# An instruction scheduler's cost table re-measured: lengths taken from spacings in the trace, a port charge and table loads counted in an operation's length

## The chip, the cores and the metric

The kernel runs on one core of a Trainium2 chip. The core has five engines, each with its own queue, worked off strictly in order: TensorE (matrix products), VectorE, ScalarE (activation functions), GpSimd, and SyncE, which here only issues DMA transfers. In profiles they are called PE (and PEld for the loading of stationary operands), DVE, ACT, POOL and SP. The metric is the device time of one execution in microseconds, taken as the median over several runs.

## The reference

A two-layer model on 256 tokens of width 1024, all in fp32. Each layer is: half a gated feed-forward block, a mixer, half a feed-forward block, each with a root-mean-square norm before and after it:

```python
for i in range(DEPTH):
    g = norm_g[i]
    h = h + 0.5 * rms_norm(swiglu(rms_norm(h, g[0]), ffn_w1[i, 0], ffn_w2[i, 0]), g[1])
    u = rms_norm(h, g[2])
    m = conv_ssd_mixer(...) if i % 2 == 0 else dilated_attention_mixer(...)
    h = h + rms_norm(m, g[3])
    h = h + 0.5 * rms_norm(swiglu(rms_norm(h, g[4]), ffn_w1[i, 1], ffn_w2[i, 1]), g[5])
```

The feed-forward width is 2816. Layer 0's mixer is a hybrid. One branch is `silu(layer_norm(conv31(val * sigmoid(gate))))`, with a depthwise convolution over 31 tokens and 1024 channels. The other is a state-space branch with 16 heads of 64 and two chunks of 128 tokens: a convolution over 4 tokens, softplus step sizes, products masked by exponential decays, and a gate `silu(z)`. Both are joined by one output product. Layer 1's mixer is attention with 8 heads in three dilation groups, merged by their softmax sums.

## The kernel before, in words

**Stages.** `run` (L1165) records six stages one after another: feed-forward, hybrid mixer, feed-forward, feed-forward, attention, feed-forward. Activations are kept transposed (`xT`), in two tiles of 128 tokens. Every large product is made of three passes: each operand is split into a high part, rounded to the fp32r format (ScalarE writes it, named `wh` for weights), and a remainder (`wl`, a subtraction on VectorE), and `mm3` and `feat_major` multiply high by high, high by low and low by high.

**Weights.** They stream in units of 128x2048 (1 MB): SyncE loads `raw`, ScalarE copies it to `wh`, VectorE subtracts to `wl`. Units 38 to 60 (`GPSIMD_UNITS`, L44), which belong to the hybrid mixer and the start of the next feed-forward block, have the subtraction on GpSimd in pieces of 512 columns instead (L542). There are 4 buffers each for `raw`, `wh` and `wl`.

**The hybrid mixer** (`hybrid`, L787) has the most kinds of work. The long convolution (`long_conv`, L806) is 240 `scalar_tensor_tensor` operations on VectorE that accumulate into two PSUM banks, `t` and `c`, in two groups; they are the taps. They are recorded 2000 places later than they stand in the program (L821), so VectorE fills with them. Next to them run the step sizes (`step_sizes`, L750: some 16 operations on 32 columns that end in tile `a`, with two Exp activations), the decays (`decays`, L875: a mask product on GpSimd, a matmul, Exp on ScalarE, a product on VectorE; for the first chunk also small copies into `left`), the state-space products, and their normalization (the scaling `v<-v,m,g`). At the end the convolution's result goes through a layer norm over channels, from L988 on: products with a tile `mean`, squares, 32 one-column products, a power on GpSimd, two products that spread the result, Silu, a split, and then the last big products.

**Order of issue.** Nothing is issued as it is written. `Recorder` takes down all operations with their dependences and then makes a list schedule (`schedule`, L317). It keeps, for each engine, the time at which it becomes free, and for each operation the time at which its inputs are ready. For each engine `choose` (L346) looks at all operations that could start: the start `s` is the later of those two times, and later still if a buffer has no place yet. Among the operations that could start within `LOOK` of the earliest one (50 ns on TensorE, 100 on VectorE and ScalarE, 0 on GpSimd and SyncE, L425) it takes the one with the lowest rank, its place in the program. Of all engines' choices the one with the earliest start is issued, and its length, `o.cost`, is added (L390). `cost` (L429) has the lengths, in ns, by engine, operation and size; `latency` (L463) the delay from one operation's end to the start of one that needs it. So a length decides nothing by itself: it moves the times at which others can start, and with them the order in each queue, the GpSimd pieces' places in it, and which buffer each tile is given. All instructions are issued from one line, L418, which is therefore the line of nearly every row of the profile.

Of the kernel before, what the change touches and what calls it, by code (L numbers as in the profile page):

```python
# [17 lines left out]
P = 128  # L18
# [30 lines left out]

# ---------------------------------------------------------------- weight order  # L50
def _unit_a(cols512):
# [113 lines left out]

# ------------------------------------------------------------ order of issue
class View:
    """A region of a buffer that has no place yet: the path of view operations, and the region it names in the first buffer of its kind."""

# [23 lines left out]
    def pieces(self):  # L193
        """The parts of the buffer it touches."""
        dims = self.ap.ap[1:]
        at = np.array([self.ap.offset % self.buf.cols])
        for step, n in dims:
            at = (at[:, None] + step * np.arange(n if step else 1)).ravel()
        return np.unique(at // self.buf.grain).tolist()
# [18 lines left out]
class Kind:  # L218
    """Buffers of one size that take turns in the same places."""

# [24 lines left out]
class Recorder:  # L245
    """Takes the program down, then issues it engine by engine in the order of a list schedule."""

# [61 lines left out]
    @contextmanager  # L309
    def moved(self, ranks):  # L310
        """What is recorded inside counts as so many places later."""
        before = self.offset
        self.offset += ranks
        yield
        self.offset = before

    def schedule(self):  # L317
# [28 lines left out]
        def choose(e):  # L346
            found = []
            low = None
            for o in cands[e]:
                s = max(free[e], ready[o.index])  # L350
                if e == "scalar" and o.table and o.table != table:
                    s += TABLE_LOAD
                for b in o.bufs:
                    if b.slot is None:
                        t = place_time(b)
                        if t is None:
                            break
                        s = max(s, t + GAP)
                else:
                    found.append((o.rank, s, o))  # L360
                    if low is None or s < low:
                        low = s
            if low is None:
                return None
            return min((f for f in found if f[1] <= low + LOOK[e]), key=lambda f: f[:2])

        while len(order) < len(ops):
# [11 lines left out]
            for b in o.bufs:  # L379
                if b.slot is None:  # L380
# [8 lines left out]
                    b.last = 0.0  # L389
            free[e] = s + o.cost  # L390
            if e == "sync":
                bus = max(bus, s + DMA_START) + o.tail
                end[o.index] = bus + DMA_LATENCY
            else:
                end[o.index] = s + o.cost
            o.start, o.end = s, end[o.index]
# [23 lines left out]

TABLE_LOAD = 1300.0
GAP = 100.0
# [6 lines left out]
def cost(op, out):  # L429
    """Time on the engine, in ns, and for a transfer its time on the wires."""  # L430
    kw = op.kw
    op.table = None
    n = out.free_size() if isinstance(out, View) else 0
    if op.engine == "tensor":
# [3 lines left out]
        if stationary.ap.dtype == F32R:  # L438
            return max(n, 256) / 2.4 + 2.5, 0.0
        return max(2 * n, 2 * stationary.free_size()) * 2 / 2.4, 0.0  # L440
    psum = any(isinstance(a, View) and a.buf.kind.psum for a in (*op.args, *kw.values()))
# [4 lines left out]
    if op.engine == "gpsimd":  # L446
        if op.name == "memset":
            return 100.0, 0.0
        return (464.0 if n == 1 else 2.15 * n + 60.0), 0.0
    if op.engine == "vector":  # L450
        if op.name == "tensor_scalar" or op.name == "tensor_copy":
            return (0.52 if not psum else 1.04) * n + (70.0 if n < 64 else 130.0), 0.0
        if op.name == "scalar_tensor_tensor":
            return 1.03 * n + (130.0 if n > 64 else 75.0), 0.0
        if op.name == "tensor_reduce":
            n = op.kw["in_"].free_size()
# [11 lines left out]

# --------------------------------------------------------------------- program
class Kernel:  # L470
# [33 lines left out]

    # ---- storage
    def keep(self, name, shape, dtype=F32):
# [19 lines left out]

    # ---- weights
    def split(self, hi, lo, src, engine=None):
# [28 lines left out]

    # ---- matrix products: a, b are (hi, lo) pairs
    def mm3(self, out, a, b, start, stop):
# [38 lines left out]
    def to_transposed(self, src, hi_of, lo_of, n, banks="tc", gain=None):  # L598
        """src: list of [P, 512] token-major pieces; transposes n blocks into split operands."""
        nc = self.nc  # L600
# [18 lines left out]

    # ---- norms  # L620
    def rstd(self, sums, eps):
# [11 lines left out]
    def post_pre(self, t, y, half, gpost, gpre, xT, last=False):  # L633
        """h += f * rms(y) * gpost, then the transposed split of rms(h) * gpre."""
        with self.nc.moved(-HURRY):
# [31 lines left out]

    # ---- gated pairs: func(first) * second
    def gated_tok(self, xT, func, consume, bank="t", first=False):
# [30 lines left out]
    def gated_feat(self, xT, func):  # L700
        """[feature block, token] products of one pair of units."""
        first, second = self.unit(256), self.unit(256)
# [7 lines left out]

    # ---- ffn
    def ffn(self, xT, done):
# [35 lines left out]

    # ---- hybrid mixer
    def step_sizes(self, xT):  # L750
        """softplus step sizes and their decays, [token, (chunk, head)]."""
        nc = self.nc
# [34 lines left out]
    def hybrid(self, xT, done):  # L787
# [4 lines left out]

        # input of the long depthwise convolution, [channel, token]
        glu = []
# [41 lines left out]

        # short convolutions of the state-space branch, [channel, token]
        def xbc_pair(j):
# [16 lines left out]

        # decays between tokens of a chunk, [source, head, target], and score masks
        after, upto = self.order[:, 0, :], self.order[:, 1, :]
        cb = self.slot([P, NT, 2, P])
        for t in range(NT):
# [3 lines left out]
            V.tensor_tensor(out=cb[:, t], in0=pc, in1=upto.unsqueeze(1).to_broadcast([P, 2, P]), op=ALU.mult)  # L863
        # B of the first chunk, [token, state], and the decay since the start of the second
        pb, pg = self.ps([P, 2, P], "a"), self.ps([P, 16], "a")
# [36 lines left out]

        # inputs of the state-space branch, [token, channel]
        xs = [[None, None] for _ in range(NT)]
# [15 lines left out]

        # gate z, [token, channel]; outputs per chunk and group; the state after the first chunk feeds the second
        zu = [[self.unit(512), self.unit(512)] for _ in range(2)]
# [61 lines left out]

        # layer norm of the long convolution over channels
        pm, pv, pr = (self.ps([P, n], tag) for n, tag in zip((SEQ, NT, SEQ), LN_BANKS))
# [42 lines left out]

    # ---- attention mixer  # L1030
    def attention(self, xT, done):
# [216 lines left out]
```

## Time and profile before

| | |
|---|---|
| median of 3 runs | 1151.29 us (1149.3 to 1154.03) |
| span of the profiled execution | 1150.6 us |
| mean granted TensorE clock | 0.992 |
| instructions | 17628, of them 7192 matmuls |
| table loads on ScalarE | 14 |

The span is from the profiled execution's first to its last instruction; the profile states no other time of that execution. In the rows, an instruction is written as engine, line, operation, output tile, inputs, and shapes; names such as `w`, `a`, `t`, `c` are PSUM tiles, and `cv`, `s`, `pt`, `v`, `m` tiles in SBUF. In a view by stretches each engine's busy microseconds stand in the order of its heading, with the number of instructions behind them. In the timeline a row starts with its start and length in microseconds; what stands in brackets is the engine's idle time before it and what ended it. In a view of waits the numbers are the total, the times and the longest. In groups the numbers behind the bar are the busy time, the mean duration in ns, and idle time before. Durations overlap a little from one instruction to the next, so that the spacing of a series is shorter than the duration of one.

### The profile page before, as it was taken

The page shows a single profiled execution, that of the slowest core. Times are in us where ns is not written, and L with a number is a line of the kernel's source. Part 1 is how long each engine was busy: PE and PEld are TensorE (multiplying, and loading weights), DVE is VectorE, ACT ScalarE, POOL GpSimd, SP SyncE. Part 2 cuts the span into 40 slices and gives each one's busy share as a digit, 9 for nine tenths or more (in the row PEclk, how much of TensorE's full clock was granted, in tenths as well). Part 3 has the DMA queues.
Part 4 walks back from the last instruction along what each step waited for, and adds up shares of the span by engine and source line. Part 5 has one row for each costly group of instructions (what it writes and reads, how often), then busy time and mean ns, then how long its engine had stood idle before and what let it go on. Part 6 is the DMA issues. An engine that isn't in the chain of part 4 may idle for free.

```text
span 1150.6 us, 17628 instructions
## 1 busy us (share of the span) xinstructions
PE 1111.9 (97%) x7192; PEld 997.6 (87%) x7192; DVE 689.4 (60%) x1085; ACT 570.0 (50%) x960; POOL 161.8 (14%) x147
## 2 busy tenths in 40 slices
PE   6999999999999899999999999999999999999997
PEld 5899998798777678999988999998999987999996
DVE  5645446799899376355468455458556457554553
ACT  7634435656754455344455344445565566444442
POOL 0000000378887420000000000001000000000000
PEclk9999999999999799999999999999999999999999
DMA  9755454535324346555546555555634413655521
GB/s 333 267 184 183 163 204 147 196 134 186 108 82 159 112 179 219 183 183 179 189 147 238 202 190 180 187 183 175 235 110 154 147 73 125 224 181 185 189 105 37
DMA packets 29921, 197.21 MB, mean 171 GB/s; under 512 B 3600, under 2 KB 4496, under 8 KB 7312
## 3 DMA queue, kind: packets, MB, share of 16 engines
q1 hardware_dynamic: 29840, 196.09, 48.6%
q8 instruction: 56, 0.92, 0.3%
q14 instruction: 25, 0.20, 0.1%
HBM read 195.03 MB, written 1.05 MB: 170 GB/s over the span
## 4 chain that ended last, share of the span: by engine, by line
PE 61%; DVE 1%; ACT 1%; issue 1%; POOL 0%; DVEq 0%; POOLq 0%; ACTq 0%
PE w L418 40%; PE a L418 19%; PE t L418 1%; PE c L418 1%; ACT s L418 0%; ACT wh L418 0%; DVE wl L418 0%; DVE y L418 0%; ACT junk L418 0%; POOL m L418 0%; DVE h L418 0%; DVE x L418 0%; DVE s L418 0%; ACT x L418 0%; POOL wl L418 0%
## 5 line engine op out<-in xcount | busy, mean ns | idle before, releaser
L418 DVE TENSOR_TENSOR wl<-raw,wh 128x1024 fp32r<-128x1024 f32 x310 | 371.5, 1226 | 268.9 <-ACT wh L418 268.7
L418 PE MATMUL w<-x,wh 128*128 128x256 f32 x2912 | 528.0, 283 | 0.9 <-DVE pt L418 0.6
L418 ACT ACTIVATE wh<-raw 128x1024 fp32r<-128x1024 f32 (+1 forms) x402 | 367.3, 955 | 255.7 <-PE w L418 152.3
L418 PEld LDWEIGHTS w<-x,wh 128*128 128x128 f32 x2912 | 454.6, 191 | 5.2 <-issue 1.0
L418 PE MATMUL w<-x,wl 128*128 128x256 f32 x1456 | 412.1, 283 | 0.0
L418 PEld LDWEIGHTS w<-x,wl 128*128 128x128 f32 x1456 | 278.2, 191 | 0.3 <-issue 0.3
L418 PE MATMUL a<-wh,s 128*128 128x512 f32 x768 | 248.2, 397 | 2.0 <-ACT s L418 2.0
L418 PEld LDWEIGHTS a<-wh,s 128*128 128x128 f32 x768 | 145.1, 189 | 35.5 <-ACT s L418 2.7
L418 PE MATMUL w<-wh,x 128*128 128x512 f32 x480 | 156.1, 400 | 4.8 <-ACT x L418 2.7
L418 PE MATMUL a<-wl,s 128*128 128x512 f32 x384 | 151.9, 395 | 0.0
L418 POOL TENSOR_TENSOR m<-m,mhalf 128x1 f32<-128x1 f32 (+1 forms) x27 | 19.2, 712 | 930.0 <-DVE m L418 930.0
L418 POOL TENSOR_TENSOR wl<-raw,wh 128x512 fp32r<-128x512 f32 x92 | 118.9, 1332 | 39.1 <-ACT wh L418 36.2
L418 PEld LDWEIGHTS w<-wh,x 128*128 128x128 f32 x480 | 90.7, 190 | 27.3 <-ACT x L418 3.6
L418 ACT ACTIVATE sg<-w 128x256 f32<-128x256 f32 x96 | 36.3, 378 | 156.7 <-PE w L418 156.7
L418 PE MATMUL w<-wl,x 128*128 128x512 f32 x240 | 95.0, 397 | 0.9 <-POOL wl L418 0.9
L418 DVE TENSOR_TENSOR cv<-sg,w 128x256 f32<-128x256 f32 x76 | 31.8, 418 | 94.0 <-ACT sg L418 94.0
L418 PEld LDWEIGHTS a<-wl,s 128*128 128x128 f32 x384 | 72.6, 189 | 15.6
L418 DVE SCALAR_TENSOR_TENSOR t<-cv,chan,t 128x255 f32<-128x255 f32 (+29 forms) x120 | 56.0, 466 | 3.5 <-ACT t L418 3.1
L418 DVE SCALAR_TENSOR_TENSOR c<-cv,chan,c 128x255 f32<-128x255 f32 (+29 forms) x120 | 55.9, 466 | 0.3 <-ACT c L418 0.2
L418 PEld LDWEIGHTS w<-wl,x 128*128 128x128 f32 x240 | 45.6, 190 | 11.3 <-POOL wl L418 1.7
L418 DVE TENSOR_TENSOR y<-a,g 128x512 f32<-128x512 f32 x24 | 16.4, 684 | 37.1 <-ACT junk L418 37.1
L418 ACT ACTIVATE s<-cv 128x512 fp32r<-128x512 f32 (+1 forms) x44 | 25.6, 594 | 16.0 <-DVE cv L418 16.0
(132 smaller groups left out, 733.7 us busy)
## 6 DMA issues: line engine op xcount, KB each, us to landing
raw<-in_weights SPq DMA_DIRECT2D x176, 1024.0 KB, 4.9
g<-in_gains SPq DMA_DIRECT2D x12, 512.0 KB, 4.3
raw<-in_weights SPq DMA_DIRECT2D x4, 512.0 KB, 8.6
h<-in_x SPq DMA_DIRECT2D x2, 512.0 KB, 6.2
out<-h SPq DMA_DIRECT2D x4, 256.0 KB, 2.1
s<-in_consts SPq DMA_DIRECT2D x3, 192.0 KB, 2.4
chan<-in_chan SPq DMA_DIRECT2D x1, 166.0 KB, 8.5
order<-in_consts SPq DMA_DIRECT2D x1, 128.0 KB, 9.3
```

Of the source, the lines that this page charges most:

```text
L418: o.ins = f(*[real(a) for a in o.args], **{k: real(a) for k, a in o.kw.items()})
```

## The change

Only `schedule` and `cost` change in effect (the rest of the diff removes comments and docstrings). In `schedule`, the test for a table load no longer delays the start of an operation in `choose`; it stands where the chosen operation's length is worked out. An operation of VectorE that has no PSUM operand (`shares_port`) gets, also after it has been chosen, the rest of the GpSimd operation that the plan has running at its start. In `cost`, the lengths of fp32r and fp32 products, GpSimd operations, and `scalar_tensor_tensor` without a pointer are new; `bn_stats` and `bn_aggr` do not occur in this kernel.

```diff
@@ choose
                 s = max(free[e], ready[o.index])
-                if e == "scalar" and o.table and o.table != table:
-                    s += TABLE_LOAD
@@ schedule
-            free[e] = s + o.cost
+            length = o.cost
+            if e == "scalar" and o.table and o.table != table:
+                length += TABLE_LOAD
+            if o.shares_port:
+                length += max(0.0, free["gpsimd"] - s)
+            free[e] = s + length
             if e == "sync":
                 bus = max(bus, s + DMA_START) + o.tail
                 end[o.index] = bus + DMA_LATENCY
             else:
-                end[o.index] = s + o.cost
+                end[o.index] = s + length
@@
-TABLE_LOAD = 1300.0
+TABLE_LOAD = 1294.0
@@ cost
     op.table = None
+    op.shares_port = False
@@ tensor
         if stationary.ap.dtype == F32R:
-            return max(n, 256) / 2.4 + 2.5, 0.0
-        return max(2 * n, 2 * stationary.free_size()) * 2 / 2.4, 0.0
+            return n / 2.4 + 17.0 if n > 256 else 120.0, 0.0
+        return 2 * max(2 * n / 2.4 + 2.5, 112.0), 0.0
@@ gpsimd
-        return (464.0 if n == 1 else 2.15 * n + 60.0), 0.0
+        if n == 1:
+            return 515.0, 0.0
+        return (2.35 if out.ap.dtype == F32R else 1.9) * n + 40.0, 0.0
     if op.engine == "vector":
+        op.shares_port = not psum
@@ scalar_tensor_tensor
-            return 1.03 * n + (130.0 if n > 64 else 75.0), 0.0
-        if op.name == "tensor_reduce":
+            return 1.03 * n + (130.0 if n > 64 and isinstance(kw.get("scalar"), View) else 75.0), 0.0
+        if op.name == "bn_aggr":
+            return 200.0, 0.0
+        if op.name in ("tensor_reduce", "bn_stats"):
             n = op.kw["in_"].free_size()
```

Between the choice and these lines stands, unchanged, L377 and 378: `if e == "scalar" and o.table: table = o.table`.

## The prediction

> **What bounds the kernel now.** I read the page's head first, then busy time by stretches of the span, then the waits of TensorE and VectorE inside the stretch that stood out, then the timeline there.
>
> ```profile
> span 1150.6 us, 17628 instructions
> PE 1111.9 (97%) x7192; PEld 997.6 (87%) x7192; DVE 689.4 (60%) x1085; ACT 570.0 (50%) x960; POOL 161.8 (14%) x147
> ```
> ```profile
> core 0: us, PE busy (x) PEld busy (x) DVE busy (x) ACT busy (x) POOL busy (x), PEclk, DMA share, GB/s
> 0.00:25.00 25.00, 15.25 (x60) 11.75 (x61) 15.12 (x31) 17.55 (x36) 1.56 (x8) 1.00 0.89 320
> 25.00:205.00 180.00, 180.00 (x1204) 165.38 (x1203) 96.12 (x111) 85.99 (x117) 1.10 (x2) 1.00 0.55 194
> 205.00:225.00 20.00, 19.00 (x89) 15.24 (x88) 13.26 (x23) 11.52 (x22) 4.34 (x4) 1.00 0.62 214
> 225.00:373.20 148.20, 137.95 (x859) 117.71 (x857) 141.40 (x336) 84.54 (x159) 121.18 (x100) 0.99 0.39 136
> 373.20:392.00 18.80, 14.08 (x54) 11.68 (x54) 8.32 (x25) 9.68 (x26) 9.96 (x9) 0.64 0.48 169
> 392.00:425.00 33.00, 30.45 (x138) 24.00 (x137) 19.57 (x31) 16.29 (x39) 13.42 (x12) 1.00 0.32 122
> 425.00:825.00 400.00, 399.93 (x2616) 364.74 (x2615) 221.22 (x266) 186.88 (x263) 6.09 (x8) 1.00 0.55 192
> 825.00:970.00 145.00, 140.91 (x1011) 126.49 (x1010) 85.90 (x166) 83.28 (x209) 3.04 (x4) 1.00 0.36 126
> 970.00:1144.00 174.00, 174.00 (x1176) 160.65 (x1174) 85.55 (x94) 73.19 (x94) 0.55 (x1) 1.00 0.44 155
> ```
>
> TensorE is idle for 1150.6 - 1111.9 = 38.7 us in all. The three feed-forward stretches (25 to 205, 425 to 825, 970 to 1144) have 0.07 us of that between them: there TensorE is the only bound, and an order can lose time but not win any. Of the rest, 9.75 us are the start (0 to 25) and 6.3 the end. What an order can win lies in the hybrid mixer: 1.0 us in 205 to 225, 10.25 in 225 to 373, 4.7 in 373 to 392, 2.55 in 392 to 425; and in the attention mixer, 4.1. In 225 to 373 VectorE is even busier than TensorE, 141.40 of 148.20 us. That stretch ends where the long convolution does:
>
> ```profile
> 369.99 1.89 PE L418 MATMUL w<-cv,mean 128*128 128x256 f32 x8
> 372.74 0.46 DVE L418 SCALAR_TENSOR_TENSOR c<-cv,chan,c 128x226 f32<-128x226 f32 x1
> 373.39 1.99 PE L418 MATMUL w<-cv,mean 128*128 128x256 f32 x8 [1.51 <-ACT cv L418]
> 387.74 0.79 PE L418 MATMUL a<-wh,s 128*128 128x512 f32 x1 [2.01 <-ACT s L418]
> ```
>
> VectorE's last tap runs at 372.74; only then can TensorE take the second half of the channel means (373.39), and a serial layer norm follows until the next big product at 387.74. TensorE's other products had run out at 369.99. So two things set when the layer norm starts: VectorE's total until the last tap, and, 3.4 us earlier, TensorE's supply of other work. The layer norm itself is the same operations in the same chain, and its granted clock was 0.64.
>
> **The change, part by part.** No operation is added, removed or resized: 7192 matmuls, 1085 VectorE, 960 ScalarE and 147 GpSimd instructions stay. The order of each queue and the place of each buffer may move, and all of the cost or gain comes from that.
>
> *Matmul lengths.* From the chain of waits:
>
> ```profile
> 462.61 11.50 PE w L418 x96
> 474.11 5.59 PE a L418 x24
> ```
>
> 11.50/96 = 119.8 ns for a 256-column product and 5.59/24 = 232.9 ns for a 512-column one. The old plan used 256/2.4 + 2.5 = 109.2 and 215.8; the new one 120 and 230.3. So the old plan let TensorE run 8 to 9% too fast against engines whose lengths were about right. In 225 to 373 that is an estimated 137.95 x 0.085 = 11.7 us over the stretch. An engine's queue is strict in order, so an operation planned too early holds up what is ready behind it. On VectorE what is behind it is nearly always a tap of the convolution. What this cost so far is in VectorE's waits of that window:
>
> ```profile
> DVE s L418 <- ACT s L418: 3.1, 4, 1.4
> DVE t L418 <- ACT t L418: 3.1, 2, 2.8
> ```
>
> These two are 6.2 of the 148.20 - 141.40 = 6.8 us that VectorE is idle there. If the plan is right, taps fill such gaps and the last tap comes up to 6.8 us earlier; if it is not, nothing comes. I take 5, since the 3.1 us on t is the start of a group of taps, which partly stays. TensorE must then run out of other work earlier as well; it has 10.25 us of idleness in the window, of which these two are the largest:
>
> ```profile
> PE a L418 <- ACT s L418: 3.8, 3, 2.8
> PE w L418 <- DVE pt L418: 2.3, 3, 0.9
> ```
>
> 5 us more on VectorE asks for 5 - 3.4 = 1.6 of those 10.25: not the limit.
>
> *GpSimd lengths and the port.*
>
> ```profile
> 222.60 15.01 POOL L418 TENSOR_TENSOR wl<-raw,wh 128x512 fp32r<-128x512 f32 x12 [11.72 <-ACT wh L418]
> 234.68 2.98 DVE L418 SCALAR_TENSOR_TENSOR m<-m 128x32 f32<-128x32 f32 x1
> 244.00 4.04 POOL L418 TENSOR_TENSOR s<-m,order 128x512 f32<-128x512 f32 x4 [6.39 <-DVE m L418]
> 275.57 2.51 DVE L418 COPY m<-s 128x4 f32<-128x4 f32 x1
> 278.73 0.16 DVE L418 COPY m<-s 128x4 f32<-128x4 f32 x1
> L418 DVE TENSOR_TENSOR s<-s,s 128x512 f32<-128x512 f32 x8 | 8.3, 1067 | 1.2 <-ACT s L418 0.7
> 278.12 0.69 DVE L418 TENSOR_TENSOR s<-s,s 128x512 f32<-128x512 f32 x1
> L418 DVE SCALAR_TENSOR_TENSOR v<-v,m,g 128x512 f32<-128x512 f32 x4 | 6.9, 1765 | 0.2
> L418 DVE SCALAR_TENSOR_TENSOR h<-y,m,h 128x512 f32<-128x512 f32 x24 | 17.1, 748 | 1.5
> ```
>
> A weight piece takes 15.01/12 = 1.25 us on GpSimd; the old plan had 2.15 x 512 + 60 = 1.16, the new one 2.35 x 512 + 40 = 1.24. A mask product takes 4.04/4 = 1.01; old 1.16, new 1.9 x 512 + 40 = 1.01. The held operations are real: 2.98 us for 32 columns, over as GpSimd's batch ends (222.60 + 15.01 = 237.61); a copy of 2.51 against 0.16; eight decay products at 1.067 against 0.69; four scalings at 1.765 against 0.748. Together (2.98 - 0.2) + (2.51 - 0.16) + 8 x 0.38 + 4 x 1.02 = 12.2 us of VectorE's 141.40. But the change puts this into the length, after the choice: VectorE still takes such an operation when its rank says so, and still stands. I take 0 for these 12.2 us. Bounds: all gone, -12; as much again, +12.
>
> The plan's charge is also not what happens. It runs to the end of the GpSimd operation in progress, at most 1.24 us, while the copy stood 2.35 longer than its twin, through two boundaries of a batch. And it falls on every operation without a PSUM operand, where this one ran freely inside a batch:
>
> ```profile
> 350.22 2.53 POOL L418 TENSOR_TENSOR wl<-raw,wh 128x512 fp32r<-128x512 f32 x2
> 351.12 0.20 DVE L418 TENSOR_SCALAR m<-m 128x1 f32<-128x1 f32 x1
> ```
>
> The Trainium skill (GPSIMD Engine Reference, Key points) limits the contention to VectorE instructions in a 2-port mode or with two SBUF inputs, which speaks against charging the rest. The row of 0.20 us agrees with it, and by it the sum is the same.
>
> *Table loads.* Here the code does not do what the change's name says. The line `table = o.table` (L378) stands between the choice and the new lines and was not moved. When the length is worked out, `o.table != table` is therefore always false, and no load is ever charged. The start no longer holds it either. So in the new plan a load costs nothing, neither in the choice between two operations nor in time.
>
> ```profile
> L418 ACT ACT_TABLE_LOAD x14 | 18.0, 1283 | 8.4 <-DVE s L418 4.2 <-PE a L418 3.3 <-PEq L1238 0.7
> 272.78 0.55 ACT L418 ACTIVATE s<-w,chan 128x256 f32<-128x256 f32 x1
> 273.35 1.28 ACT L418 ACT_TABLE_LOAD   x1
> 274.64 0.18 ACT L418 ACTIVATE m<-a 128x16 f32<-128x16 f32 x1
> 287.10 1.28 ACT L418 ACT_TABLE_LOAD   x1 [3.63 <-DVE s L418]
> 313.93 1.28 ACT L418 ACT_TABLE_LOAD   x1 [3.27 <-PE a L418]
> ```
>
> A switch costs 274.64 - 273.33 = 1.31 us, and what follows one is now planned that much too early. Where ScalarE has work before the load, its slack (148.20 - 84.54 = 64 us in the hybrid's long stretch) takes it up. Where ScalarE had been waiting for the input, as at 287.10 and 313.93, the load lies on a chain, and the engine that comes next stands for it: TensorE waits 3.8 us for s in this window (the row above). I take three such places, 3 x 1.3 = +4. Then the number of loads: the old rule kept a function of another table behind any copy that could start within 1.2 us; now rank alone decides, and Exp and Silu may alternate. Two loads fewer would be -2.6; four more, all on a chain, +5.2; I take 0. The feed-forward stretches use Silu alone, attention Exp alone; one Exp (of `heads`, L773) runs in the first feed-forward block, where TensorE never waits, and may move into the start, where it does: -1.3 to +2.6, taken as 0.
>
> The Trainium skill (ScalarE: Activation LUTs, What ACT_TABLE_LOAD costs) adds a drain of 1.38 us to each switch and comes to about 2.66. The trace disagrees with its 1.31. By the page the three places would be +8 instead of +4.
>
> *The small ones.* fp32 products get 2 x 112 ns where they had 213, scalar_tensor_tensor without a pointer 75 ns where it had 130; power 515 for 464. They shift attention and layer norm by tens of ns each. Attention's stretch is idle for 4.1 us in many short waits; I take 1 of it (bounds 0 to 3 gained, 3 lost). At 392 to 425, where the gated h returns to the feed-forward, I take 1 of 2.55. SyncE's queue holds the same loads; it works on at most 0.62 of the DMA engines' time outside the start (205 to 225), so loads that move by a few us stay covered. The start stays: its waits are on loads and on the first normalization. The feed-forward stretches stay at 0; should a weight piece come late there, nothing covers it, since TensorE has no slack.
>
> Sum against the profiled execution: 1150.6 - 5 + 4 - 1 - 1 = 1147.6. The median of the runs, 1151.29, lies 0.7 above the span, so 1148.3; I say 1148.5. That is less than the 5.75 us (0.5%) that a measurement of this kernel can tell from no change.
>
> **Rivals.** *Faster, by the right pace.* If the free table loads cost nothing because ScalarE's slack takes them all up, the sum is 1144.3. If then TensorE still has products left when the layer norm starts, they cover part of its 4.7 us of idleness in 373 to 392, and some of the time at clock 0.64: another 4, so 1140. For it: 8 to 9% on every product is no rounding, and a TensorE that is planned right moves every queue. Against it: VectorE idles only 4.6% of its stretch, and 12.2 us of its time are port waits that no choice looks at. I put it at 1142.
>
> *Slower, by the port.* Step sizes and decays need some 16 tiny VectorE operations in a row, nearly all without PSUM. So far only the first was held (2.98), since GpSimd then stood idle 6.39 us, waiting for their result. The new plan makes that chain longer, by up to 1.24 us each, and GpSimd takes whatever starts earliest: if it has weight pieces to put into that gap, each tiny operation stands for one. Half a piece for all 16 is 16 x 0.62 = 10 us more on VectorE, which moves the last tap and the layer norm by as much: 1151.3 + 10 = 1161. It decides from about 9 of them held. For it: all of that can be seen in the rows above. Against it: the weight pieces need free buffers, which the old order lacked at 237.61.
>
> *Slower, by free table loads.* If Exp and Silu alternate in the hybrid, eight more loads, half of them on a chain, are 4 x 1.3 = 5.2 beside the 4 above, and the pace gains nothing: 1151.3 + 9 = 1160. It decides from about 18 loads in all. Against it: ranks keep the Exps of one chunk together.
>
> *Nothing done.* The issued orders could come out nearly the same, since ranks make most choices: 1151. With so many ties in time I give that little, inside the forecast's case.
>
> **How the numbers follow.** The forecast, gains and losses that nearly cancel, from 1145.5 to 1157: 0.38. Faster, 1136 to 1145.5: 0.33. Slower, 1157 to 1168: 0.29, of which 0.17 by the port and 0.12 by the loads. The likeliest case's own range is 1145.5 to 1157. The range over all, 1137 to 1164, leaves out about 0.05 below, where the port waits would have to go too, and 0.1 above.
>
> **What would show it.** Right: TensorE still without idleness in the feed-forward stretches; VectorE's idle time before the last tap under 4 us, the last tap at 369 to 373, a layer norm as long as before; longer waits behind two or three table loads. Wrong: the last tap before 366 or after 377; held tiny operations in a row between the step sizes and the decays; more than 16 loads; idleness of TensorE in a feed-forward stretch.

## The result and the profile after

| | before | after |
|---|---|---|
| median | 1151.45 us (4 runs, 1149.3 to 1154.03) | 1162.55 us (4 runs, 1162.23 to 1163.66) |
| span of the profiled execution | 1150.6 us | 1161.9 us |
| mean granted TensorE clock | 0.992 | 0.987 |
| table loads on ScalarE | 14 | 16 |

The ratio is 1.0112, with a 95% interval of 1.0093 to 1.013: 1.1% slower. The head of the page after:

```profile
span 1161.9 us, 17647 instructions
PE 1115.7 (96%) x7192; PEld 997.1 (86%) x7192; DVE 688.5 (59%) x1085; ACT 573.4 (49%) x962; POOL 158.6 (14%) x147
```

The engines do the same work as before, within 4 us each; TensorE's idle time went from 38.7 to 46.2 us. Where it is, the view by stretches of the changed kernel tells, cut at the same events as before:

```profile
core 0: us, PE busy (x) PEld busy (x) DVE busy (x) ACT busy (x) POOL busy (x), PEclk, DMA share, GB/s
25.00:205.00 180.00, 180.00 (x1206) 165.20 (x1205) 97.88 (x112) 86.38 (x116) 1.09 (x2) 1.00 0.55 196
205.00:225.00 20.00, 18.59 (x86) 14.65 (x85) 12.70 (x22) 10.79 (x22) 3.20 (x4) 1.00 0.56 201
225.00:378.83 153.83, 138.82 (x860) 117.63 (x858) 141.58 (x336) 88.49 (x162) 123.81 (x103) 0.99 0.39 138
378.83:400.00 21.17, 16.46 (x53) 13.43 (x54) 8.31 (x25) 9.88 (x27) 6.39 (x6) 0.50 0.30 101
432.00:832.00 400.00, 399.59 (x2612) 363.06 (x2611) 221.91 (x265) 185.60 (x259) 4.93 (x8) 1.00 0.55 194
832.00:981.00 149.00, 140.66 (x1012) 126.41 (x1011) 86.08 (x166) 83.54 (x209) 3.04 (x4) 1.00 0.35 124
981.00:1155.50 174.50, 174.50 (x1179) 160.28 (x1177) 85.52 (x94) 73.25 (x94) 0.55 (x1) 1.00 0.44 154
```

The feed-forward stretches are as full as they were (399.59 of 400, 174.50 of 174.50). Two places are longer. From 225 to the last tap it is 153.83 us where it was 148.20, and VectorE, with the same 336 instructions and nearly the same work (141.58 against 141.40), idles 12.25 us in place of 6.8. In attention TensorE idles 8.3 us in place of 4.1. In the timeline the end of the convolution and the layer norm:

```profile
378.37 0.44 DVE L421 SCALAR_TENSOR_TENSOR c<-cv,chan,c 128x226 f32<-128x226 f32 x1
379.01 3.78 PE L421 MATMUL w<-cv,mean 128*128 128x256 f32 x8 [5.09 <-ACT cv L421]
395.53 0.79 PE L421 MATMUL a<-wh,s 128*128 128x512 f32 x1 [2.01 <-ACT s L421]
```

The last tap comes at 378.37 (372.74 before), TensorE stands 5.09 us for it (1.51 before), and the first big product behind the layer norm is at 395.53 (387.74). From the second means to that product it is now 16.5 us instead of 14.35, at a granted clock of 0.50 in 378.83 to 400. What VectorE waits for ahead of the last tap (total, times, longest):

```profile
DVE t L421 <- ACT t L421: 5.0, 2, 2.8
DVE m L421 <- ACT s L421: 4.0, 3, 1.8
DVE s L421 <- ACT s L421: 2.7, 3, 1.4
```

The second row is new: 4.0 us in which `m` waits for `s` of ScalarE. And in attention, two waits of TensorE for the copy of `cv`, where before had one of 0.33 us at 895.61:

```profile
865.37 0.51 PE L421 MATMUL w<-x,wh 128*128 128x256 f32 x2 [1.48 <-ACT cv L421]
903.27 0.50 PE L421 MATMUL w<-x,wh 128*128 128x256 f32 x2 [1.59 <-ACT cv L421]
```

The new row of VectorE, seen close up. ScalarE, TensorE and VectorE of the changed kernel:

```profile
271.62 1.28 ACT L421 ACT_TABLE_LOAD   x1
273.15 1.12 PE L421 MATMUL a<-s,order 128*128 128x512 f32 x2 [1.39 <-ACT m L421]
274.31 0.60 ACT L421 ACTIVATE s<-a 128x512 f32<-128x512 f32 x1 [0.18 <-PE a L421]
274.93 1.28 ACT L421 ACT_TABLE_LOAD   x1
274.94 1.94 DVE L421 COPY m<-s 128x4 f32<-128x4 f32 x1 [1.81 <-ACT s L421]
276.22 0.63 ACT L421 ACTIVATE s<-s 128x512 f32<-128x512 f32 x1
276.87 1.28 ACT L421 ACT_TABLE_LOAD   x1
276.90 1.16 PE L421 MATMUL a<-s,s 128*128 128x128 f32 x8 [0.93 <-ACT s L421]
278.16 0.60 ACT L421 ACTIVATE s<-a 128x512 f32<-128x512 f32 x1
278.81 3.68 PE L421 MATMUL a<-s,order 128*128 128x512 f32 x4 [0.75 <-ACT s L421]
280.89 0.60 ACT L421 ACTIVATE s<-a 128x512 f32<-128x512 f32 x1 [2.13 <-PE a L421]
281.52 0.17 DVE L421 COPY m<-s 128x4 f32<-128x4 f32 x1 [1.52 <-ACT s L421]
283.16 0.17 DVE L421 COPY m<-s 128x4 f32<-128x4 f32 x1 [0.64 <-ACT s L421]
```

A Silu (`s<-s`) stands between the Exps (`s<-a`) of one chunk, so that three loads fall into 6.5 us. The plan holds them to be free. TensorE stands behind each of them: 1.39 us for the small Exp after the first load (ScalarE's `m`), 0.93 for the Silu after the second, 0.75 for the Exp after the third. The granted clock in 278.8 to 282.5 was then 0.54, and four products with `order` took 3.68 us. The Exps need these products (at 280.89 ScalarE itself has waited 2.13 us for one), and VectorE's copies need the Exps; the plan has set them only 0.1 to 2.5 us behind the ends that it gives the Exps without loads. So VectorE stands at three copies, 1.81 + 1.52 + 0.64 = 3.97 us; the taps behind them could have run. The loads reach it for the greater part by way of TensorE.

### The profile page after: what moved, and what is told of

Same layout as the page of the kernel before. It is cut to its first block, busy times and chain, and to the rows that moved or that the text cites. A ratio compares the mean times of both kernels' runs of the same rounds, so it can differ in the third digit from the quotient of the medians.

```text
span 1161.9 us, 17647 instructions
## 1 busy us (share of the span) xinstructions
PE 1115.7 (96%) x7192; PEld 997.1 (86%) x7192; DVE 688.5 (59%) x1085; ACT 573.4 (49%) x962; POOL 158.6 (14%) x147
## 4 chain that ended last, share of the span: by engine, by line
PE 58%; DVE 3%; ACT 2%; issue 1%; POOL 1%; DVEq 0%; POOLq 0%; ACTq 0%
PE w L421 38%; PE a L421 18%; ACT s L421 1%; PE t L421 1%; DVE y L421 1%; ACT wh L421 1%; DVE h L421 0%; POOL m L421 0%; PE c L421 0%; DVE s L421 0%; DVE x L421 0%; ACT junk L421 0%; DVE wl L421 0%; DVE m L421 0%; POOL wl L421 0%
## 5 line engine op out<-in xcount | busy, mean ns | idle before, releaser
L421 PEld LDWEIGHTS w<-wl,x 128*128 128x128 f32 x240 | 45.7, 191 | 12.2 <-DVE wl L421 1.4
```

Of the source, the lines that this page charges most:

```text
L421: o.ins = f(*[real(a) for a in o.args], **{k: real(a) for k, a in o.kw.items()})
```

## The experiments

Two measures recur. *Lost time* of TensorE is its start-to-start spacings, less what the same shape took in the median of the trace of before; for a single wait that is nearly the bracket in the row. *Planned* times are the starts and ends that the kernel's own list schedule gave its operations; they are no measurements, but they can be laid beside the trace, operation by operation.

The first question was whether the uncounted table loads alone make the loss, or the new product lengths, or the port charge, or whether any new order costs about as much.

**The product lengths alone.** The kernel before, with

```diff
-            return max(n, 256) / 2.4 + 2.5, 0.0
-        return max(2 * n, 2 * stationary.free_size()) * 2 / 2.4, 0.0
+            return n / 2.4 + 17.0 if n > 256 else 120.0, 0.0
+        return 2 * max(2 * n / 2.4 + 2.5, 112.0), 0.0
```

> The kernel before with the new matmul lengths alone (fp32r and fp32). Theory 'free loads': 14 loads; the pace by itself does no harm, 1146 to 1153 (my prediction took -5 to -7 for it). Rival 'lengths': 1157 to 1163, with VectorE's idle time before the last tap over 10 us and attention's 3.8 us with it. Rival 'port charge': 1149 to 1154.

Measured: 1160.66 us, ratio 1.0093 (1.0063 to 1.0123). The last tap came at 365.8, 7 us earlier than before, VectorE waited nowhere for ScalarE's `s` for more than 0.2 us in all, and the kernel was slower nevertheless. TensorE took the means only at 372.71:

```profile
372.71 3.62 PE L418 MATMUL w<-cv,mean 128*128 128x256 f32 x16
```

All 16 in a row and no wait before them: TensorE was the late one. Ahead of them it stood for other things, 10.6 us in 225 to 374.4; in the kernel before these other things were 8.9 us, since 1.51 of its 10.44 us up to 373.4 were the wait for the tap. Between the two profiled executions (before's was a long one in the hybrid, as the last section shows) only 1.0 of the 7.1 us were lost up to the second half of the means. 0.6 followed in the layer norm, 2.9 between it and the first scores of attention, and 1.6 between attention's scores.

**The free table loads alone.** The kernel before without the load in the start:

```diff
-                if e == "scalar" and o.table and o.table != table:
-                    s += TABLE_LOAD
```

> The kernel before, with one edit: choose no longer adds the table load to the start (so loads are free in the plan, as in the changed kernel; all lengths are the old ones). Theory 'free loads' (the Exps of the first chunk are parted by a Silu at 275 us, VectorE's copies stand behind them, the last tap comes 5.6 us later, the layer norm 7.8): 16 loads, waits of VectorE's m on ScalarE's s of about 4 us, last tap 376 to 379, 1157 to 1163. Rival 'lengths' (the new matmul lengths move the queues against each other): 1149 to 1154, last tap within 1.5 us of 372.7. Rival 'port charge': as the rival 'lengths' here.

Measured: 1150.44 us, ratio 1.0001 (0.9985 to 1.0018). 16 loads as in the changed kernel, and VectorE's waits for `s` grew from 3.1 to 5.3 us, but the time did not move. Alone, on the old lengths, free loads cost nothing that can be measured.

**The port charge alone.** The kernel before with `shares_port` and its charge in the length:

```diff
+            if o.shares_port:
+                length += max(0.0, free["gpsimd"] - s)
```

> The kernel before with the port charge alone added to the length of VectorE's operations without PSUM. Theory 'free loads': 1149 to 1154. Rival 'lengths': 1149 to 1154. Rival 'port charge': 1157 to 1163, with more held VectorE operations than before (12.2 us).

Measured: 1152.45 us, ratio 1.0025 (1.0013 to 1.0038).

**The change without free loads.** The changed kernel with the old test back in `choose`, so that a load delays the start again:

```diff
                 s = max(free[e], ready[o.index])
+                if e == "scalar" and o.table and o.table != table:
+                    s += TABLE_LOAD
```

> The changed kernel with the table load back in the start in choose; all the new lengths and the port charge stay. Theory 'free loads': 14 loads, no Silu between the Exps, last tap 369 to 374, 1145 to 1153 (attention's 3.8 us, which have no load in them, may stay: then 1152 to 1155). Rivals 'lengths' and 'port charge': 1159 to 1164.

Measured: 1159.71 us, ratio 1.0088 (1.0053 to 1.0122). The last tap came back to 371.7, and nearly four fifths of the loss stayed. So neither the loads nor any other single part explains the whole, and the parts do not add up: 0.93, 0.01 and 0.25% alone.

The next question was whether the planned pace of TensorE as such does it: a plan that lets TensorE run too fast gives everybody else a lead.

**The change with the old product lengths**, the first diff reversed in the changed kernel.

> The changed kernel with the old matmul lengths (256/2.4 + 2.5 and so on); port charge, free loads and the rest stay. Theory 'matmul lengths' (the right pace itself makes the order worse): 1148 to 1154. Rival 'any new order' (the old order is a lucky one, every change of lengths draws another, usually 0 to 12 us slower): anything from 1149 to 1163.

Measured: 1165.76 us, ratio 1.0138 (1.0113 to 1.0164), above both ranges. TensorE stood 17.5 us for the last tap:

```profile
387.75 3.78 PE L421 MATMUL w<-cv,mean 128*128 128x256 f32 x8 [17.50 <-ACT cv L421]
```

and VectorE had waited ahead of it mostly for ScalarE's `s`:

```profile
DVE s L421 <- ACT s L421: 9.9, 10, 2.8
```

So the new product lengths are no plain harm. Put into the kernel before they lose 0.93%; among the other parts of the change the kernel is no slower with them than without (1.0112 against 1.0138, intervals that overlap).

**The pace alone.** The kernel before with one factor on the length of fp32r products: 0.915, 1.01 and 1.18.

```diff
-            return max(n, 256) / 2.4 + 2.5, 0.0
+            return (max(n, 256) / 2.4 + 2.5) * 0.915, 0.0
```

> The kernel before with its fp32r lengths times 0.915 (99.9 ns for 256 columns), so that the plan is as wrong again as it was. Theory 'matmul lengths', in the form that a TensorE planned too fast gives the operations behind it a head start in their queues: 1147 to 1153. Rival 'any new order': 1149 to 1163, likely 1155.

> The kernel before with its fp32r lengths times 1.01, an error that nobody could call one. Theory 'head start': 1150 to 1153. Rival 'any new order': 1153 to 1160, since the order of the queues differs in many places.

> The kernel before with its fp32r lengths times 1.18 (128.8 ns for 256 columns against 119.8 on the chip): TensorE is planned too slow. Theory 'head start': 1164 to 1175, with TensorE idle in the transitions between feed-forward blocks and in attention. Rival 'any new order': 1149 to 1163, no worse than the changed kernel.

Measured: 1161.5 us (ratio 1.0097, 1.0072 to 1.0123) for 0.915, 1148.78 (0.9991, 0.9979 to 1.0004) for 1.01, 1175.27 (1.0216, 1.0187 to 1.0246) for 1.18. The last taps were at 382.9, 368.7 and 371.3. No line can be drawn through this: the old pace is at or near a good place, both sides of it are worse, and the time follows neither the pace nor the last tap. A simple head start of TensorE is not the cause.

Laying plan and trace beside each other brought the next theory. The wait for the second half of the means stands in the plans themselves, nearly as long as on the chip. Planned and then lost: before 2.55 and 1.77, changed 5.36 and 5.35, the port alone 11.07 and 10.32, old product lengths in the changed kernel 18.55 and 17.76, the new product lengths alone 0 and 0; the fast pace is the one that is off, 12.13 and 8.50. So it might be that the lengths are now right, the trace does what is planned, and what is planned is a worse order. Four kernels, all made from the changed one, tried that.

**Without the port charge:**

```diff
-            if o.shares_port:
-                length += max(0.0, free["gpsimd"] - s)
```

> The changed kernel with the port charge taken out again; the new lengths and the uncharged table loads stay. So far the wait of TensorE for the second half of the channel means (w<-cv,mean, released by ScalarE's cv) has stood in the plan of every kernel nearly as long as on the chip: before 2.55 planned and 1.77 measured, changed 5.36 and 5.35, the port alone 11.07 and 10.32, old product lengths with the rest 18.55 and 17.76, the new lengths alone 0 and 0. Theory one, the plan itself holds the lost time (exact lengths, a worse order): this plan has no wait there (0 instead of 5.36), VectorE's last tap 10.6 us earlier in the plan; so on the chip that wait is under 0.6, the layer norm starts 4 to 6 us earlier, the two attention waits of 1.65 and 1.75 stay because they stay in the plan (1.50 and 1.60), and the time is 1156 to 1160. Theory two, the loss comes from what the plan does not know: the uncounted VectorE-GpSimd waits add to the uncounted loads, VectorE is idle over 12 us before the last tap, 1162 or more.

Measured: 1167.24 us, ratio 1.0154 (1.0131 to 1.0177). The wait at the means did vanish, as planned; but the tap came at 377.5, not 10 us earlier, TensorE was later still (it took the first half of the means at 382.19), and VectorE stood at many places:

```profile
DVE s L419 <- ACT s L419: 4.3, 3, 1.6
DVE t L419 <- ACT t L419: 4.0, 2, 2.8
DVE m L419 <- ACT s L419: 2.1, 2, 1.4
DVE x L419 <- ACT x L419: 1.7, 1, 1.7
```

In the hybrid mixer the second theory was right: what the plan does not know costs.

**With loads counted in the length**, as the change's name has it: the two lines that note the table move behind the test.

```diff
-            if e == "scalar" and o.table:
-                table = o.table
...
                 length += TABLE_LOAD
+            if e == "scalar" and o.table:
+                table = o.table
```

> The changed kernel with a table load really counted in the length (the line table = o.table moved behind the test). Theory one: planned wait at the second half of the means 1.02 instead of 5.36, layer norm planned 1.9 longer, both attention waits kept; planned end 2.5 us earlier, so 1158.5 to 1161. Theory two, the uncounted loads are what costs: VectorE's copies behind a Silu between two Exps no longer stand (4 to 5 us less idle on VectorE before the last tap), layer norm as before, 1154 to 1157.

Measured: 1152.77 us, ratio 1.0022 (1.0007 to 1.0036). That takes back four fifths of the loss, with two moved lines, and still with 16 loads. The time is below the second theory's range. VectorE's waits for `s` are gone from the view; its longest row is

```profile
DVE t L421 <- ACT t L421: 3.1, 2, 2.8
```

and the same place in the timeline:

```profile
272.80 0.46 DVE L421 SCALAR_TENSOR_TENSOR c<-cv,chan,c 128x234 f32<-128x234 f32 x1
273.39 1.28 ACT L421 ACT_TABLE_LOAD   x1
275.33 1.28 ACT L421 ACT_TABLE_LOAD   x1
276.72 1.93 PE L421 MATMUL a<-s,order 128*128 128x512 f32 x4
277.27 0.16 DVE L421 COPY m<-s 128x4 f32<-128x4 f32 x1
278.15 0.16 DVE L421 COPY m<-s 128x4 f32<-128x4 f32 x1
278.95 0.16 DVE L421 COPY m<-s 128x4 f32<-128x4 f32 x1
368.14 1.99 PE L421 MATMUL w<-cv,mean 128*128 128x256 f32 x8 [0.96 <-ACT cv L421]
```

The loads come just as close together, at 271.37, 273.39 and 275.33. But now VectorE has eight taps in its queue from 272.80 on, while ScalarE loads, and the copies stand behind them and wait for nothing. TensorE has other products in its queue there too: it waits for none of the three loads, and four products with `order` take 1.93 us. Its waits for ScalarE's `s` and `m` up to the second half of the means are 0.9 us, against 5.2 in the changed kernel. It is not the loads that cost, but queues of TensorE and VectorE that do not expect them.

**Loads counted, no port charge, and the old length of `scalar_tensor_tensor`:** the last two diffs together, and

```diff
-            return 1.03 * n + (130.0 if n > 64 and isinstance(kw.get("scalar"), View) else 75.0), 0.0
+            return 1.03 * n + (130.0 if n > 64 else 75.0), 0.0
```

> The changed kernel with loads counted in the length, no port charge and the old scalar_tensor_tensor length: the shortest plan of those that have the new product lengths (6.1 us less than the changed kernel's plan). Theory one: no wait at the means, one attention wait instead of two, 1154 to 1158. Theory two: the port waits that are not planned undo what the loads give, 1160 or more. Either way it should stay above the kernel before (1149 to 1151), since the waits left in attention are in the plan.

Measured: 1160.88 us, ratio 1.0098 (1.008 to 1.0117), 8 us more than with the charge, though its plan is the shortest of the six below. The last tap came no later than with the charge (367.20 against 367.25). TensorE was late, with the first half of the means at 374.18 against 365.29. The same stretch in this kernel, and in the one with the charge (fix):

```profile
225.00:367.70 142.70, 132.68 (x826) 113.80 (x825) 136.42 (x336) 77.95 (x148) 111.18 (x92) 0.96 0.40 136
225.00:367.70 142.70, 136.01 (x858) 116.89 (x856) 138.15 (x336) 86.46 (x161) 119.94 (x98) 1.00 0.41 141
```

TensorE is idle 3.3 us longer in the first and has made 32 products fewer; its granted clock was 0.96, not 1.00, which is an estimated 0.04 x 142.7 = 5.7 us of its work at most. Up to attention this kernel differs from the one with the product lengths alone (1160.66) in GpSimd's lengths and in where a load is counted, and its time is the same. GpSimd's new lengths were not tried by themselves.

With these kernels the surprise can be counted, for the six that have the new product lengths. The stretches are from the first product with `wdth` to the last tap, and to TensorE's second half of the means:

| | loads counted | port counted | tap, planned us | tap, measured us | means, planned us | means, measured us | excess at the means |
|---|---|---|---|---|---|---|---|
| fix | yes | yes | 130.3 | 137.8 | 131.1 | 138.7 | 7.6 |
| off_loads | yes | yes | 134.5 | 142.7 | 135.1 | 143.4 | 8.2 |
| on_matmul | yes | no | 123.0 | 135.9 | 130.2 | 144.5 | 14.3 |
| three_off | yes | no | 123.1 | 137.0 | 130.2 | 145.7 | 15.5 |
| changed kernel | no | yes | 134.8 | 148.4 | 135.5 | 149.0 | 13.5 |
| off_port | no | no | 124.2 | 147.3 | 130.1 | 153.8 | 23.7 |

The measured tap alone does not follow the time: on_matmul and three_off have it as early as fix. The measured start of the second half of the means does: the six profiled spans (1150.7, 1155.6, 1157.7, 1158.7, 1161.9 and 1167.5 us) lie in its order. There a plan that knows both is wrong by 7.6 to 8.2 us, one that lacks either by 13.5 to 15.5, one that lacks both by 23.7. These are single executions, which can differ by 3.7 us (last section), so the 15 to 16 for both is firm and the 5 to 8 for each less so; it is what carries the explanation of the hybrid. The planned column moves too, by 4.0 us between the two orders that know both, and that is the luck of the order. The rival that any new order costs some 0 to 12 us is not excluded for a single kernel; it does not say why the excess follows what the plan knows in all six.

**The `scalar_tensor_tensor` length alone undone**, the last diff in the changed kernel. It changes the planned order in attention only.

> The changed kernel with scalar_tensor_tensor without a pointer back at its old length of 130 ns over the columns' time instead of 75. Planned order before attention is the same instruction for instruction on every engine, so up to the first attention scores nothing may move. In the plan the first of attention's two waits of w<-x,wh for ScalarE's cv (1.50 planned, 1.65 measured at 865.37) is gone and the second (1.60 planned, 1.75 at 903.27) stays. Theory one: the same on the chip, 1.3 to 1.7 us less lost between the first and the last scores, and 0.5 to 0.6 of it given back behind them, so 1161.5 to 1162. Theory two, attention waits because its lengths are wrong on the chip: both waits stay.

Measured: 1160.0 us, ratio 1.009 (1.007 to 1.0111), somewhat under the expected range. The first of attention's two waits is gone, the second stays:

```profile
865.70 0.51 PE L421 MATMUL w<-x,wh 128*128 128x256 f32 x2
900.57 0.51 PE L421 MATMUL w<-x,wh 128*128 128x256 f32 x2 [1.58 <-ACT cv L421]
```

TensorE lost 2.2 us between the first and the last scores, against 3.9 in the changed kernel and 0.5 before. In attention the first theory was right.

**Attention alone.** Two kernels, with a mark in the recorder for the stage: the kernel before with the new lengths for attention's operations, and the corrected one (fix) with the old lengths, and without the port charge, for them. The line of the second is shown; in the first the old lengths are for every stage but this one.

```diff
-        op.cost, op.tail = cost(op, out)
+        op.cost, op.tail = (old_cost if self.stage in (4,) else cost)(op, out)
```

> The kernel before, with the changed lengths for the operations of the attention mixer alone; choice, port and table rules and all other lengths are those of before, so that the planned order is the same on every engine up to the end of the second layer's first feed-forward block. Its plan has two waits of w<-x,wh for ScalarE's cv of 1.50 and 1.60 in attention, where the plan of before has one of 0.93. Theory one, attention's loss comes from the new lengths by way of that order and has nothing to do with the hybrid: the same two waits on the chip (1.65 and 1.75), TensorE loses 3 to 4 us more between the first and the last scores and about 1 more behind them, nothing before: 1153 to 1155.5 where before has 1150. Theory two, attention loses because of what comes to it from the hybrid (weights and buffers that arrive in another order): no loss here, 1149 to 1151.

> The changed kernel with loads counted in the length (as in the run named fix: 1152.77) and the old lengths for the operations of the attention mixer alone; the planned order is that of fix on every engine up to the end of the second layer's first feed-forward block. Theory one, the exact lengths gain in the hybrid what attention gives back: the hybrid as in fix (TensorE loses 4.7 us less ahead of the second half of the means than before), attention as before (0.2 to 0.5 us lost instead of 4.1), 1148 to 1150 us, which is 0.1 to 0.3% under the kernel before. Theory two, attention loses because of what comes to it from the hybrid: both waits stay, 1152 to 1154.

Measured: 1154.99 us, ratio 1.0053 (1.0034 to 1.0072), for the new lengths there alone; 1149.68 us, ratio 1.0005 (0.9992 to 1.0018), for the corrected kernel with the old lengths there. In the first, both waits appear (854.70 and 892.69), with nothing new ahead of them; in the second one of 0.32 is left:

```profile
854.70 0.51 PE L422 MATMUL w<-x,wh 128*128 128x256 f32 x2 [1.49 <-ACT cv L422]
```
```profile
890.76 0.50 PE L422 MATMUL w<-x,wh 128*128 128x256 f32 x2 [0.32 <-ACT cv L422]
```

TensorE lost 4.1 us between first and last scores in the first and 0.4 in the second. So attention's loss is its own, not handed down from the hybrid. The second kernel is as fast as the kernel before, and not faster: no version here beats it by more than the measurement can tell.

## Why the prediction was wrong

It said 1148.5 us, less than 0.5% off; it is 1162.55, 1.1% slower.

*Where time can be lost.* Right: nearly everything happened in the hybrid mixer, its layer norm and attention; the feed-forward stretches stayed full. Of its signs of being wrong, the last tap after 377 came (378.37); VectorE's idle time before it was 12.25 us and not under 4. The layer norm, forecast as long as before, took 16.5 us in place of 14.35. The eight products of the second means alone, behind the longer wait, are 3.78 - 1.99 = 1.8 of that.

*Product lengths, -5.* This step failed. It took VectorE's idle time before the last tap as the thing to win and held TensorE's supply to be no limit. With the product lengths alone the taps came 7 us earlier, more than forecast, and TensorE was then not ready for them: it reached the means at 372.71, later than before (369.99). The step had also misread TensorE's slack. Of the 3.4 us between 369.99 and 373.39 the first half of the means takes 1.89, so that only the wait of 1.51 was free, and 5 us asked 3.5 more of TensorE, not 1.6. In the corrected kernel with attention's old lengths the tap was at 367.7 and the wait under 1 us, and the time was still that of before (1.0005). And the stretch itself was a long one in that execution: the kernel with the new lengths in attention alone has before's order up to there, and took 144.47 us from 225 to the last tap, not 148.20. VectorE idled 6.2 us in place of 6.8; the rest is busy time, 138.32 us in place of 141.40, since its operations were held less. That there was little to win could not be read from one trace.

*Port, 0.* Right in what it said of the held time: 8 x 0.38 us for the decay products, 4 x 0.74 for the scalings, 2.3 for the first step-size operation and 1.8 for the copies are some 10 us, where 12.2 were. Wrong in taking the charge as of no effect. Beside the new product lengths, leaving it out made the kernel slower: 1.0154 against 1.0112 with free loads, 1.0098 against 1.0022 with counted ones (there together with the `scalar_tensor_tensor` length, which in the plans moves nothing ahead of attention). Alone on the old lengths it cost 0.25%. The rival in which the tiny step-size operations are held in a row did not happen: behind the first of them, each took 0.17 to 0.35 us, as before.

*Table loads, +4.* The code was read rightly, loads are free in this plan, and this is the step that was undersized most: counting them takes 1162.55 to 1152.77, 9.8 us. The step looked for chains of ScalarE and the engine that comes next, at 1.3 us each, and such chains are there: TensorE stood 1.39, 0.93 and 0.75 us behind three loads, 3.1 us where the step took 3.9. What it left out is what follows from them: products at half the clock, and VectorE's queue, where a copy that comes too early holds up the taps behind it. The rival with free loads named 1160 and this mechanism's root, but it wanted about 18 loads for it; there were 16, and the corrected kernel has 16 too. Why the same freedom costs nothing on the old product lengths (1.0001) is open: VectorE's waits for `s` grew there by 2.2 us only, and two executions of one order differ by more than that.

*Attention, -1.* Wrong in sign: TensorE lost 3.4 us more between the scores and some 1.2 more at the turn behind them. It was argued that right lengths fill small gaps. They put the transposes and the products for the next group elsewhere, and the plan that came out has two waits of 1.50 and 1.60, which could have been read from it before anything ran; the chip lost 1.65 and 1.75. The other small term, -1 where the gated `h` returns to the feed-forward, was right: TensorE's idle time there went from 2.55 us (392 to 425) to 0.83 (400 to 432).

The sum, with the trace's numbers for the corrected steps: up to the second half of the means TensorE lost 22.3 us before and 28.3 after, in the layer norm 6.3 and 8.5, in attention with its turn 5.2 and 9.9. That is 6.0 + 2.2 + 4.7 = 12.9, against 11.3 us by which the spans differ; the rest are small differences of either sign elsewhere. Against another execution of before's order (last section) the hybrid's part would be some 3.7 us larger.

## What to carry to other kernels

A greedy list schedule does not get better with every true length: compare the idle time that the old and the new plan themselves hold, place by place, before running either, since here it foretold the waits at the means and in attention, in all orders but one within 1 us. Then lay plan and trace beside each other, because what the plan leaves out (here table loads and the shared port, 5 to 8 us each) is paid for where a strict queue expects a result too early. Look for it on every engine: an early last tap was worth nothing where TensorE came late. And when a rule moves from the choice into the length, look at which line updates its state first.

## What the runs showed of the hardware

Two executions of one order differed in where GpSimd held VectorE. The kernel before, and the one with the new lengths in attention alone, have the same VectorE order up to 889 us; two tiny instructions of the step sizes in the second of them:

```profile
234.97 0.46 DVE L422 SCALAR_TENSOR_TENSOR m<-m 128x32 f32<-128x32 f32 x1
235.47 1.20 DVE L422 TENSOR_SCALAR m<-m 128x32 f32<-128x32 f32 x1
```

Before, the first took 2.98 us and the second 0.18. With a few more such places the last tap came 3.7 us earlier, at 369.0, with nothing changed ahead of it. The Trainium skill (SBUF — State Buffer, SBUF: two separate sides) says that of a GpSimd instruction and a VectorE instruction in a 2-port mode or with two SBUF inputs, whichever starts first has the shared ports for its whole instruction. The 1.20, less than one of GpSimd's pieces of 1.25 us, fits that; the 2.98 does not, since it lasted over more than one piece.

VectorE can hold GpSimd as well. In the kernel before, GpSimd's power takes 0.55 us at one turn and 1.40 at another, where VectorE's subtraction of a weight with two inputs runs:

```profile
607.70 0.55 POOL L418 TENSOR_TENSOR m<-m,mhalf 128x1 f32<-128x1 f32 x1 [6.22 <-DVE m L418]
611.17 1.40 POOL L418 TENSOR_TENSOR m<-m,mhalf 128x1 f32<-128x1 f32 x1 [2.92 <-DVE m L418]
610.94 1.22 DVE L418 TENSOR_TENSOR wl<-raw,wh 128x1024 fp32r<-128x1024 f32 x1
```

And a wait of TensorE costs again after it ends. The eight products of the second means took 1.99 us behind a wait of 0.96 or 1.51, 3.64 behind one of 3.80 (the change without free loads), and 3.78 behind one of 5.09, 10 or 17.5. The Trainium skill (TensorE: Matmul & The Clock Gate, What's actually happening) puts the change to half the clock at an idle window of about 3.4 us; these waits agree, with a granted clock of 0.50 behind the one of 5.09. But shorter ones can do it too: in the changed kernel the clock was 0.54 in 278.8 to 282.5, behind waits of 1.39, 0.93 and 0.75, and four products took 3.68 us that take 1.93 in the corrected kernel.
